# Products of odd chunks in the other half of the array, and key norms spread by a repeated stationary column

## The chip, the cores and the metric

The kernel runs on one core of a Trainium2 chip. The time is the device time of one launch in microseconds (us). Before the change three runs took 1141.73, 1145.06 and 1147.56 us; the median is 1145.06 us. A difference of about 0.5% (5.7 us) is what a measurement of this kernel can tell from no change.

Engines are named as the profile names them: PE is TensorE's matmul side and PEld its weight loads, DVE is VectorE, ACT is ScalarE, POOL is GpSimd, SP issues most of the DMAs. All of them work through their own instructions strictly in order.

## What is computed

The reference is a two-layer network on one sequence of 256 tokens of width 2048: an RWKV-7 layer, then an attention layer with compressed, selected and windowed keys. The change lies in the RWKV layer. Cut to what matters there:

```python
rkvz = jnp.einsum('nbtd,nde->nbte', mixed[:4], w_rkvz)
r, k, v, z = rkvz[0], rkvz[1], rkvz[2], rkvz[3]
kk = heads(k * k_k)
kk = kk / jnp.maximum(jnp.sqrt(jnp.sum(kk * kk, axis=-1, keepdims=True)), 1e-12)
k = k * (1.0 + (a - 1.0) * k_a)
o = wkv7_scan(rh, heads(decay), kh, vh, -kk, kk * ah)
```

`wkv7_scan` is a recurrence over the tokens with a 64 x 64 state for each of 32 heads. The kernel computes it in chunks of 64 tokens: four chunks (NCH = 4), and per head and chunk a 64 x 64 matrix of products between the normed, decayed keys and their scaled counterparts, of which a triangular inverse is needed.

## The kernel before

Weights come from HBM as fp32 pieces (`wraw`), and each is split into a high and a low part (`whi` by ACT at L211, `wlo` by DVE, some by POOL, at L190); three matmuls per weight block then give nearly fp32 products. PE is busy with these dense products almost throughout. A weight buffer has five places, so `whi` and `wlo` of a unit are made some four units ahead of the matmuls that read them, and not earlier than PE has let go of an old place.

The program runs in stages. First v, then one column block z0, then the sixteen key blocks k0 to k15 of 128 channels (two heads each), then z1 to z3, then the scan over the chunks together with the products for r. The change lies in the stage of the key blocks. Behind the dense products of key block j, a side chain `stage_k(j)` makes what the scan needs from it. In its order: two small matmuls for decay and gate (L689, L690); a copy and a square of the block (L695, L696) and the sums of the squares of the two heads by matmul into columns 256 to 259 of a PSUM bank `rn` (L699); `sst`, the floor of the sums, on DVE (L707); `rnt`, the power -1/2, on POOL (L708); then the norms have to be spread from one column per head over 64 partitions: ACT writes each norm 64 times side by side (`rnx`, L714, 128 x 256) and PE transposes that in two 128 x 128 blocks into `rn` (L717). DVE reads `rn` for `nk` (L729), then makes `at` (L730, a part of the tile `sp`) and `an` (L731). POOL makes the four parts of BK in `sp` (L736, L737). `sp` goes to HBM (`spd`, L739), PE makes eight 64 x 64 products, one per chunk and head (L744), ACT evicts them (`abs`, L746) and one DMA on SP writes them to HBM (`abd`, L747).

In the products, head 0 lies in partitions 0 to 63 and head 1 in 64 to 127, for the operands and for the output. So one product works in the upper left quarter of the array and the next in the lower right one.

When block 7 has been written, a side program `stage_t(0)` starts (`inverse_ops`): it loads eight blocks of products from `abd` (tile `invA`, two DMAs at L780) and computes triangular inverses with many small DVE operations, all of line L774 (tiles `invT`, `invM`, `invX`). The second half of the blocks follows in the scan. Another side program mixes the inputs for r (`mtmp` at L433, the two parts of `mx` at L426 and L427), also on DVE and ACT. z1 is closed by a tanh on ACT and a product on DVE (`zth`, L647), which frees a PSUM bank that z2 needs: z2 takes the two banks 2 and 0, and bank 0 is one of z1's.

Up to the scan the instructions are put in order by a scheduler that simulates the engines when the program is built: side chains are woven into the dense stream where it expects their inputs to be there. From the scan on, a planner written in the kernel sets the order.

Of the kernel before, what the change touches and what calls it, by code (L numbers as in the profile page):

```python
# [12 lines left out]
AF = mybir.ActivationFunctionType  # L13
# [211 lines left out]
def hybrid_kernel(ctx: ExitStack, tc: tile.TileContext, a: dict, out: bass.AP):  # L225
    nc = tc.nc
    V, S, G, PE = nc.vector, nc.scalar, nc.gpsimd, nc.tensor
# [147 lines left out]
    ident = C("ident")  # L375
# [286 lines left out]
    abd = dram.tile([16, NCH, 2, 128, 32], F32, name="abd")  # L662
# [11 lines left out]
    c3 = lambda x: x.rearrange("p (c t) -> p c t", c=NCH)  # L674

    def stage_k(j):
        PE, V, S, G = Ranked(nc.tensor, "skPE"), Ranked(nc.vector, "skE"), Ranked(nc.scalar, "skE"), Ranked(nc.gpsimd, "skE")
        yield lambda: j in kdone and (j < KLAG or (j - KLAG) in a1done)
        tmp = lambda name, bufs=2: kph.tile([128, T], F32, name=name, bufs=bufs)
        abs_ = tmp("abs")  # L680
# [17 lines left out]
        for tt in range(2):  # L698
# [11 lines left out]
        cum = tmp("cum")  # L710
        V.tensor_tensor_scan(cum, C("rst"), thw, 0.0, op0=OP.mult, op1=OP.add)
        yield 1000.0
        rnx = tmp("rnx")
        S.activation(rnx.rearrange("p (a b n) -> p a b n", a=2, b=2),  # L714
                     rnt[:, :, :, None].to_broadcast([128, 2, 2, 64]), AF.Copy)
        for tt in range(2):
            PE.transpose(rn[:, tt * 128:(tt + 1) * 128], rnx[:, tt * 128:(tt + 1) * 128], ident)  # L717
        sch.t += 215
        G.memset(pp[:, :, 0:1], 1.0)
        S.activation(pp[:, :, 1:], c3(cum), AF.Exp, scale=-DECAY)  # L720
# [19 lines left out]
        ab = accp("ab")  # L740
        for c in range(NCH):
            for h in range(2):
                r = slice(64 * h, 64 * h + 64)
                PE.matmul(ab[r, c * 64:c * 64 + 64], c3(at)[r, c, :], BK[r, c, h, :], start=True, stop=True)  # L744
        sch.t += 700
        S.activation(abs_, ab[:, :256], AF.Copy)  # L746
        nc.sync.dma_start(abd[j].rearrange("c k p s -> p (c k) s"), abs_.rearrange("p (n s) -> p n s", s=32))  # L747
        a1done.add(j)

    kacc = []  # L750
# [314 lines left out]
    def phase(U, c, p):  # L1065
# [5 lines left out]
        if p == 0:  # L1071
            if c == 0:
                removal(U, 0)
            else:
                for k, o in enumerate((px, O)):
                    for x, h in each:
                        PE.matmul(o[H(x, h), x], ARS[U % 2][x][R[h], k, c - 1, :], st[R[h], x, :], start=False, **mm)
        elif p == 1:
            for x, h in each:
                PE.matmul(pu[R[h], x], Yb[U % 2][H(x, h), x, c, :], XS[U][H(x, h), x, :], start=False, **mm)  # L1080
        elif p == 2:
            if c < NCH - 1:
                for x, h in each:
                    PE.matmul(pS[R[h], x], BKT[U % 2][x][:, c, h, :], uv[:, x, c, h, :], start=False, **mm)
            for x, h in each:
                PE.matmul(O[H(x, h), x], AMR[U % 2][:, h, x, c, :], uv[:, x, c, h, :], start=False, **mm)
            if c < NCH - 1:
                removal(U, c + 1)
        elif p == 3:
            XS[U] = scan.tile([128, 2, 64], F32, name="X", bufs=2)  # L1090
            S.activation(XS[U], px, AF.Copy)
        elif p == 4:
            for h in range(2):
                S.activation(uv[R[h], :, c, h, :], pu[R[h]], AF.Copy)
        elif p == 5:
            nxt = scan.tile([128, 2, 64], F32, name="S", bufs=3)
            if c == 0:
                V.tensor_copy(nxt, pS)
            else:
                V.tensor_tensor(nxt, SST[U][1], pS, op=OP.add)  # L1100
            SST[U] = (nxt, None)
        else:
            nxt = SST[U][0]
            dec = scan.tile([128, 2, 64], F32, name="sP", bufs=2)
            for x in range(2):
                S.activation(dec[:, x], nxt[:, x], AF.Copy, scale=PCH[U][:, x, c:c + 1])
            SST[U] = (nxt, dec)
# [880 lines left out]
```

## Time and profile before

| | |
|---|---|
| median of three runs | 1145.06 us (1141.73 to 1147.56) |
| the profiled execution, its own time | 1145.28 us |
| its span, first to last instruction | 1143.5 us |
| mean granted TensorE clock | 0.992 |
| PE, PEld busy | 1113.6 us, 962.9 us |
| DVE, ACT, POOL busy | 864.4 us, 715.3 us, 346.9 us |
| time of the DMA packets of SP's queue | 65.0% of 16 engines' span |

In the profile every instruction has its source line. An fp32 matmul stands as two records, a transpose as one. Matmuls are pipelined: a record's duration is longer than the step from one record's start to the next, and that step is what a matmul costs in a dense stream. "Idle before" is the time in which the engine stood before the instruction, with what ended it.

### The profile page before, as it was taken

To read this page: it belongs to the slowest core of one execution; us is meant where nothing else is said; L and a number is where in the kernel's file an instruction comes from. 1 tells how busy PE (TensorE), PEld (TensorE's weight loads), DVE (VectorE), ACT (ScalarE), POOL (GpSimd) and SP (SyncE) were. 2 spreads that over 40 slices of the span, in tenths; PEclk is the share of its full clock that TensorE was granted. 3 is DMA by queue.
4 is the path that set the end of the run, shared out by engine and by line. 5 is a ranking of instruction groups with operands and counts; after the bars stand their busy time and mean duration, and the time that the engine had idled before them with its cause. 6 is when DMAs were issued, how large, how long until landed. Compare 5 with 4: busy or idle time off the path is not lost.

```text
span 1143.5 us, 24949 instructions
## 1 busy us (share of the span) xinstructions
PE 1113.6 (97%) x9136; PEld 962.9 (84%) x9136; DVE 864.4 (76%) x1807; ACT 715.3 (63%) x1680; POOL 346.9 (30%) x443
## 2 busy tenths in 40 slices
PE   8999999999999999999999999999999999999997
PEld 7788899988688988888778888787889988888787
DVE  7999976779978986556666877675576888988564
ACT  5667777767655465556556766664666666666553
POOL 1400045554434365444110010100334344452212
PEclk9999999999999999999999999999999999999999
DMA  6568978885899978665457758585756453748462
GB/s 227 169 189 233 250 205 245 227 219 173 265 282 276 240 196 236 170 172 137 139 183 224 234 166 284 164 291 167 187 152 162 117 149 105 198 108 283 166 194 102
DMA packets 238522, 225.37 MB, mean 197 GB/s; under 512 B 57541, under 2 KB 184821, under 8 KB 238400
## 3 DMA queue, kind: packets, MB, share of 16 engines
q1 hardware_dynamic: 233120, 217.17, 65.0%
q0 software_dynamic: 5280, 6.61, 2.1%
q8 instruction: 72, 1.18, 0.5%
q14 instruction: 50, 0.41, 0.1%
HBM read 200.48 MB, written 23.10 MB: 196 GB/s over the span
## 4 chain that ended last, share of the span: by engine, by line
PE 62%; DVE 5%; DMA 2%; issue 2%; ACT 1%; POOL 1%; POOLq 0%; ACTq 0%; DVEq 0%
PE bank L576 9%; PE bank L577 9%; PE bank L579 9%; PE bank L601 5%; PE bank L1285 3%; PE bank L602 3%; PE bank L241 2%; DMA Yb<-yvd 2%; PE bank L1286 2%; PE bank L1287 2%; DVE wlo L190 2%; PE pair L1304 2%; PE pair L1306 1%; PE pair L1305 1%; PE pair L241 1%
## 5 line engine op out<-in xcount | busy, mean ns | idle before, releaser
L190 DVE TENSOR_TENSOR wlo<-wraw,whi 128x512 fp32r<-128x512 f32 (+2 forms) x616 | 448.9, 744 | 150.4 <-ACT whi L211 147.8
L211 ACT ACTIVATE whi<-wraw 128x512 fp32r<-128x512 f32 (+2 forms) x664 | 402.7, 620 | 232.9 <-PE bank L579 91.7
L577 PE MATMUL bank<-wlo,mx 128*128 128x512 f32 (+3 forms) x576 | 217.8, 380 | 3.5 <-DVE wlo L190 2.6
L579 PE MATMUL bank<-whi,mx 128*128 128x512 f32 (+3 forms) x576 | 215.0, 376 | 0.0
L576 PE MATMUL bank<-whi,mx 128*128 128x512 f32 (+3 forms) x576 | 186.5, 377 | 1.3 <-ACT whi L211 0.5
L577 PEld LDWEIGHTS bank<-wlo,mx 128*128 128x128 f32 x576 | 108.7, 189 | 22.8 <-DVE wlo L190 5.4
L576 PEld LDWEIGHTS bank<-whi,mx 128*128 128x128 f32 x576 | 107.9, 189 | 19.1 <-ACT mx L1869 1.2
L579 PEld LDWEIGHTS bank<-whi,mx 128*128 128x128 f32 x576 | 108.7, 189 | 16.2 <-POOL mx L1870 0.4
L190 POOL TENSOR_TENSOR wlo<-wraw,whi 128x512 fp32r<-128x512 f32 (+2 forms) x48 | 63.1, 1316 | 110.6 <-ACT whi L211 88.7
L601 PE MATMUL bank<-mx,whi 128*128 128x512 f32 x240 | 86.8, 398 | 0.0
L595 PE MATMUL bank<-mx,whi 128*128 128x256 f32 (+1 forms) x288 | 85.0, 295 | 0.3 <-ACT mx L426 0.3
L596 PE MATMUL bank<-mx,whi 128*128 128x256 f32 (+1 forms) x288 | 82.3, 286 | 0.0
L597 PE MATMUL bank<-mx,wlo 128*128 128x256 f32 (+1 forms) x288 | 81.7, 286 | 0.0
L1285 PE MATMUL bank<-mx,whi 128*128 128x256 f32 x256 | 81.6, 319 | 0.0
L577 PE MATMUL bank<-wlo,kvh 128*128 128x512 f32 x192 | 76.9, 401 | 0.0
L579 PE MATMUL bank<-whi,kvl 128*128 128x512 f32 x192 | 76.1, 396 | 0.0
L1286 PE MATMUL bank<-mx,whi 128*128 128x256 f32 x256 | 72.9, 285 | 0.0
L1287 PE MATMUL bank<-mx,wlo 128*128 128x256 f32 x256 | 72.8, 284 | 0.0
L602 PE MATMUL bank<-mx,wlo 128*128 128x256 f32 x256 | 70.6, 285 | 0.2 <-DVE wlo L190 0.2
L576 PE MATMUL bank<-whi,kvh 128*128 128x512 f32 x192 | 67.4, 396 | 0.0
L426 ACT ACTIVATE mx<-mtmp 128x256 fp32r<-128x256 f32 x96 | 38.7, 413 | 31.1 <-DVE mtmp L433 30.8
L595 PEld LDWEIGHTS bank<-mx,whi 128*128 128x128 f32 (+1 forms) x288 | 54.0, 187 | 2.2 <-ACT mx L426 0.7
(344 smaller groups left out, 2393.8 us busy)
## 6 DMA issues: line engine op xcount, KB each, us to landing
wraw<-in_a_w_rkvz_dram SPq DMA_DIRECT2D x128, 512.0 KB, 5.4
wraw<-in_kv_w_dram SPq DMA_DIRECT2D x48, 512.0 KB, 4.4
wraw<-in_b_w_in_dram SPq DMA_DIRECT2D x40, 512.0 KB, 4.2
wraw<-in_a_w_o_dram SPq DMA_DIRECT2D x32, 512.0 KB, 4.6
wraw<-in_b_w_o_dram SPq DMA_DIRECT2D x32, 512.0 KB, 3.9
spd<-sp SPq DMA_DIRECT2D x16, 642.0 KB, 5.1
wraw<-in_b_w_in_dram SPq DMA_DIRECT2D x24, 384.0 KB, 3.4
spl<-spd SPq DMA_DIRECT2D x14, 642.0 KB, 7.2
```

Of the source, the lines that this page charges most:

```text
L190: eng.tensor_tensor(lv, src, hv.bitcast(F32), op=OP.subtract)
L211: self.nc.scalar.activation(hv, src, AF.Copy)
L576: PE.matmul(o, mh[:, ts], wh[:, 0, :], start=k == ends[0], stop=False)
L577: PE.matmul(o, mh[:, ts], wl[:, 0, :], start=False, stop=False)
L579: PE.matmul(o, ml[:, ts], wh[:, 0, :], start=False, stop=k == ends[1])
L595: PE.matmul(o, wh[:, s, :], mh, start=k == 0 and first, stop=False, **kw)
L596: PE.matmul(o, wh[:, s, :], ml, start=False, stop=False, **kw)
L601: PE.matmul(o, wh[:, s, :], joint[nm, k], start=k == 0, stop=False, **kw)
L602: PE.matmul(o[:, :T], wl[:, s, :], mh, start=False, stop=False, **kw)
L1285: PE.matmul(o, wh[:, s, :], mh, start=k == 0, stop=False)
L1286: PE.matmul(o, wh[:, s, :], ml, start=False, stop=False)
L1287: PE.matmul(o, wl[:, s, :], mh, start=False, stop=k == NK - 1)
```

## The change

The norms are spread without a copy: PE takes a norm column of `rnt`, repeated 64 times by a zero step, as the stationary operand and the identity as the moving one. Four plain fp32 matmuls (two token halves, two heads), each to 64 partitions of `rn`, stand in place of one ACT operation and two transposes. The line numbers of the changed kernel are smaller by one from here to the products, and larger by four behind them.

The products of the odd chunks 1 and 3 are written to the other half of the partitions and to columns 384 to 511 of the bank `rn` instead of `ab`. The four quarters of the array are thus used in turn. The eviction becomes two ACT operations of 128 x 128, one per bank, and the write to HBM three DMAs, because the odd chunks' heads are swapped between partition halves. In HBM the chunks now stand in the order 0, 2, 1, 3; the loads that follow keep that order, and the one place in the scan that picks a chunk's inverse is given the matching index.

```diff
         yield 1000.0
-        rnx = tmp("rnx")
-        S.activation(rnx.rearrange("p (a b n) -> p a b n", a=2, b=2),
-                     rnt[:, :, :, None].to_broadcast([128, 2, 2, 64]), AF.Copy)
         for tt in range(2):
-            PE.transpose(rn[:, tt * 128:(tt + 1) * 128], rnx[:, tt * 128:(tt + 1) * 128], ident)
+            for h in range(2):
+                PE.matmul(rn[64 * h:64 * h + 64, tt * 128:(tt + 1) * 128], rnt[:, tt, h:h + 1].to_broadcast([128, 64]), ident,
+                          start=True, stop=True)
...
         for c in range(NCH):
             for h in range(2):
-                r = slice(64 * h, 64 * h + 64)
-                PE.matmul(ab[r, c * 64:c * 64 + 64], c3(at)[r, c, :], BK[r, c, h, :], start=True, stop=True)
+                r, o = [slice(64 * i, 64 * i + 64) for i in (h, h ^ (c % 2))]
+                pc = (ab, rn)[c % 2][o, (384 if c % 2 else 0) + c // 2 * 64:]
+                PE.matmul(pc[:, :64], c3(at)[r, c, :], BK[r, c, h, :], start=True, stop=True)
         sch.t += 700
-        S.activation(abs_, ab[:, :256], AF.Copy)
-        nc.sync.dma_start(abd[j].rearrange("c k p s -> p (c k) s"), abs_.rearrange("p (n s) -> p n s", s=32))
+        S.activation(abs_[:, 0:128], ab[:, 0:128], AF.Copy)
+        S.activation(abs_[:, 128:256], rn[:, 384:512], AF.Copy)
+        for c, src, dst in ((0, 0, 0), (2, 0, 64), (2, 64, 0)):
+            n = 64 if c else 128
+            nc.sync.dma_start(abd[j, c:c + 2, :, dst:dst + n].rearrange("c k p s -> p (c k) s"),
+                              abs_[src:src + n, 64 * c:64 * c + 128].rearrange("p (n s) -> p n s", s=32))
...
-                PE.matmul(pu[R[h], x], Yb[U % 2][H(x, h), x, c, :], XS[U][H(x, h), x, :], start=False, **mm)
+                PE.matmul(pu[R[h], x], Yb[U % 2][H(x, h), x, 2 * (c % 2) + c // 2, :], XS[U][H(x, h), x, :], start=False, **mm)
```

Since the scheduler sets the order, the change also moves instructions that it does not touch. From z2's first matmul into bank 0 on, PE's order is the same in both kernels; before that it differs in where the side chains stand. Three places follow.

The first is PE in the dense products of key block 5, where the products of block 3 and the norms of block 4 are woven in (each row is one instruction or several alike; `bank` with a number is an allocation of a PSUM bank, L595 to L597 are the dense products). Before:

```order
L744 MATMUL bank_2365<-sp 64x64
L597 MATMUL bank_2216<-mx_1582,wlo 128x256
L595 MATMUL bank_2216<-mx_1601,whi 128x256
L596 MATMUL bank_2216<-mx_1601,whi 128x256
L597 MATMUL bank_2216<-mx_1601,wlo 128x256
L744 MATMUL bank_2365<-sp 64x64 x7
L595 MATMUL bank_2216<-mx_1617,whi 128x256
```

And now:

```order
L744 MATMUL bank_2374<-sp 64x64
L744 MATMUL bank_2239<-sp 64x64
L595 MATMUL bank_2222<-mx_1640,whi 128x256
L596 MATMUL bank_2222<-mx_1640,whi 128x256
L597 MATMUL bank_2222<-mx_1640,wlo 128x256
L595 MATMUL bank_2222<-mx_1658,whi 128x256
L744 MATMUL bank_2374<-sp 64x64
L744 MATMUL bank_2239<-sp 64x64
L744 MATMUL bank_2374<-sp 64x64 x2
L744 MATMUL bank_2239<-sp 64x64 x2
L715 MATMUL bank_2367<-cst,rnt 64x128 x4
```

The eight products are split one and seven before, two and six now, and the norms' matmuls (L715) follow directly on the second part. Over the sixteen blocks, the products stand in one piece three times before and six times now, and the norms directly behind products six times now.

The second place is DVE where the first inverse starts; `sst` here is that of key block 9. The row `COPY invT<-invA` is the first DVE operation that reads the loaded products. Before:

```order
L711 SCALAR_TENSOR_TENSOR cum<-cst,thw 128x256
L190 TENSOR_TENSOR wlo<-wraw,whi 128x512
L726 TENSOR_TENSOR f<-ksb,f 128x256
L707 TENSOR_SCALAR sst<-bank_3002 128x4
L190 TENSOR_TENSOR wlo<-wraw,whi 128x512 x2
L774 COPY invT<-invA 128x16
L774 TENSOR_TENSOR invM<-invA,invT 128x32
```

And now:

```order
L711 SCALAR_TENSOR_TENSOR cum<-cst,thw 128x256
L190 TENSOR_TENSOR wlo<-wraw,whi 128x512
L725 TENSOR_TENSOR f<-ksb,f 128x256
L707 TENSOR_SCALAR sst<-bank_3026 128x4
L778 COPY invT<-invA 128x16
L778 TENSOR_TENSOR invM<-invA,invT 128x32
L778 TENSOR_TENSOR invX<-invA,invT 128x32
```

Two weight splits that stood ahead of the copy now stand behind it. On SP, the two loads of `invA` stood behind the write of the products, two small weight loads and the write of `spd`; now they stand behind the three writes and one load of `wraw`, and the write of `spd` behind them.

The third place is DVE where z1 is closed (`zth`, from z1's two banks). Before:

```order
L774 TENSOR_REDUCE invT<-invX 128x8x8
L190 TENSOR_TENSOR wlo<-wraw,whi 128x512
L433 SCALAR_TENSOR_TENSOR mtmp<-xx,prm,xn 128x256
L427 TENSOR_TENSOR mx_4287<-mtmp,mx_4287 128x256
L433 SCALAR_TENSOR_TENSOR mtmp<-xx,prm,xn 128x256
L190 TENSOR_TENSOR wlo<-wraw,whi 128x512
L774 TENSOR_TENSOR invX<-invT,invM 128x512
L190 TENSOR_TENSOR wlo<-wraw,whi 128x512
L433 SCALAR_TENSOR_TENSOR mtmp<-xx,prm,xn 128x256
L647 TENSOR_TENSOR zth<-bank_3811,zth 128x512
L647 TENSOR_TENSOR zth<-bank_3812,zth 128x512
```

And now:

```order
L433 SCALAR_TENSOR_TENSOR mtmp<-xx,prm,xn 128x256
L427 TENSOR_TENSOR mx_4335<-mtmp,mx_4335 128x256
L190 TENSOR_TENSOR wlo<-wraw,whi 128x512
L778 TENSOR_TENSOR invX<-invT,invM 128x1024
L190 TENSOR_TENSOR wlo<-wraw,whi 128x512 x2
L427 TENSOR_TENSOR mx_4371<-mtmp,mx_4371 128x256
L433 SCALAR_TENSOR_TENSOR mtmp<-xx,prm,xn 128x256
L190 TENSOR_TENSOR wlo<-wraw,whi 128x512
L427 TENSOR_TENSOR mx_4410<-mtmp,mx_4410 128x256
L647 TENSOR_TENSOR zth<-bank_3853,zth 128x512
L778 TENSOR_REDUCE invT<-invX 128x8x8
L647 TENSOR_TENSOR zth<-bank_3854,zth 128x512
```

The inverse has come further by the time z1 is closed. From the copy of the second place to the first `zth` of the third, DVE has 168 operations before and 176 now; the eight more are two splits `wlo`, two `mx`, two products of 128 x 1024 for the inverse and two of its reductions. PE's order at the start of z2 is alike in both: five weight blocks into bank 2 alone, then the same five into bank 0.

## The prediction

> **What bounds the kernel now.** I read the busy time by stretches first, then the chain of waits, then the timelines of the engines at the places that these name. Busy time by stretches, with the seams where DVE changes its state:
>
> ```profile
> 220.00:235.60 15.60, 15.60 (x138) 14.52 (x138) 8.33 (x14) 11.96 (x31) 7.74 (x10) 1.00 0.95 243
> 235.60:311.80 76.20, 70.29 (x502) 59.45 (x500) 75.47 (x170) 53.65 (x128) 35.74 (x43) 1.00 0.72 212
> 311.80:320.00 8.20, 8.14 (x29) 6.56 (x30) 8.15 (x14) 3.89 (x7) 5.15 (x10) 0.79 1.08 303
> 320.00:364.00 44.00, 44.00 (x236) 38.19 (x235) 34.71 (x82) 25.91 (x45) 12.48 (x20) 1.00 0.96 279
> ```
>
> The columns are the stretch, its length, then PE, PEld, DVE, ACT and POOL, the clock, and DMA. Up to 235.6 us PE is busy throughout and DVE about half. From 235.6 to 311.8 it is the other way round: DVE is busy 75.47 of 76.20 us, PE has 5.91 us without work. From 320 to 364, where the scan starts, PE is full again. So the change, which lies between 147 and 312 us, falls into two regimes. The chain of waits says the same of the seam at 311.8 (start, length, what):
>
> ```profile
> 296.31 0.60 DVE wlo L190
> 296.91 0.33 DVE mx L427
> ...
> 301.32 1.15 DVE wlo L190
> ...
> 306.68 0.60 DVE invT L774
> ...
> 311.20 0.61 DVE zth L647
> ...
> 311.86 0.63 PE bank L576
> ```
>
> The chain comes down DVE's queue, through splits, mixing and the inverse, to `zth`, which closes z1, and there passes to PE, whose first matmul of z2 into bank 0 waits for it. It then stays with PE. Where that chain in DVE's queue begins is shown by DVE's timeline:
>
> ```profile
> 229.12 0.69 DVE L190 TENSOR_TENSOR wlo<-wraw,whi 128x512 fp32r<-128x512 f32 x1 [0.26 <-ACT whi L211]
> 231.62 0.69 DVE L190 TENSOR_TENSOR wlo<-wraw,whi 128x512 fp32r<-128x512 f32 x1 [1.80 <-ACT whi L211]
> 235.64 0.19 DVE L774 COPY invT<-invA 128x16 f32<-128x16 f32 x1 [3.33 <-DMA invA<-abd]
> ```
>
> DVE stands for 3.33 us until the products of the first eight blocks have come back from HBM. From then on it never stands. Thus the time at which z2 can go on is the landing of `invA` plus all the work that the order puts on DVE between the copy and `zth`. That sum, not PE's, is what the change must be measured by.
>
> **The change, part by part.** First PE's small groups. What a group costs the dense stream is the step from the last dense matmul before it to the second one behind it, less two dense steps of 0.12 us:
>
> ```profile
> 170.79 0.28 PE L596 MATMUL bank<-mx,whi 128*128 128x256 f32 x1
> 171.00 0.33 PE L744 MATMUL bank<-sp 64*64 64x64 f32 x2
> ...
> 171.47 0.28 PE L595 MATMUL bank<-mx,whi 128*128 128x256 f32 x1
> ...
> 171.71 0.29 PE L597 MATMUL bank<-mx,wlo 128*128 128x256 f32 x1
> 171.93 0.68 PE L744 MATMUL bank<-sp 64*64 64x64 f32 x14
> ...
> 172.76 0.28 PE L596 MATMUL bank<-mx,whi 128*128 128x256 f32 x1
> ...
> 173.46 0.28 PE L596 MATMUL bank<-mx,whi 128*128 128x256 f32 x1
> 173.58 0.38 PE L717 MATMUL bank<-cst,rnx 128*128 128x128 f32 x2
> ...
> 173.92 0.28 PE L595 MATMUL bank<-mx,whi 128*128 128x256 f32 x1
> ```
>
> Products: 0.44 us for two records, 0.81 for fourteen, so 0.38 for going into the small shape and back and 0.031 a record. The two transposes cost 0.22 us. The scan has groups in the new shapes (L1077: 64 x 64 pieces in all four quarters; L1086: 128 partitions onto 64, 64 moving columns):
>
> ```profile
> 439.86 0.28 PE L1287 MATMUL bank<-mx,wlo 128*128 128x256 f32 x1
> 440.07 0.46 PE L1077 MATMUL pair<-S,ars 64*64 64x64 f32 x16
> ...
> 440.68 0.28 PE L1286 MATMUL bank<-mx,whi 128*128 128x256 f32 x1
> ...
> 450.14 0.28 PE L1287 MATMUL bank<-mx,wlo 128*128 128x256 f32 x1
> 450.35 0.45 PE L1086 MATMUL pair<-uv,amr 128*64 128x64 f32 x8
> ...
> 450.95 0.28 PE L1286 MATMUL bank<-mx,whi 128*128 128x256 f32 x1
> ```
>
> Sixteen records over four quarters cost 0.58 us, or 0.0125 a record beyond the 0.38. By the order, the sixteen blocks' products cost before 13 x 1.25 + 3 x 0.88 = 18.9 us (split in two, or whole), and now 10 x (2 x 0.38 + 16 x 0.0125) + 6 x 0.58 = 13.1 us: 5.8 us saved. The norms are eight records of the L1086 kind with 128 moving columns. L1086 costs 0.57, or 0.024 a record at 64 columns; I double it: 0.38 + 8 x 0.048 = 0.76 us. If a record is no dearer than at 64 columns it is 0.57; if halves don't overlap and each record takes a transpose's 0.11, it is 1.26. I take 0.76, the row of its own shape scaled by the columns. Six of the sixteen groups share one way of the switch with products, 6 x 0.19 = 1.1 us. So the norms go from 16 x 0.22 = 3.5 us to 16 x 0.76 - 1.1 = 11.1. On PE the change therefore costs 7.6 - 5.8 = 1.8 us, between -1.3 and +9.8.
>
> From 235.6 to 311.8 this is covered by PE's 5.91 us without work, and it would cost its full price if that cover were gone. Up to block 7, whose write the inverse waits for, it counts: about 7/16 of it, 0.8 us.
>
> ACT loses sixteen `rnx` and gains sixteen evictions; it is busy 53.65 of 76.20 us and sets nothing here.
>
> Second, the landing of `invA`. The eviction of block 7's products on ACT, then SP's own queue:
>
> ```profile
> 222.99 0.39 ACT L746 ACTIVATE abs<-bank 128x256 f32<-128x256 f32 x1 [0.90 <-PE bank L744]
> ...
> 223.90 0.54 SPq L747 DMA_DIRECT2D abd<-abs  x1
> ...
> 227.94 0.35 SPq L739 DMA_DIRECT2D spd<-sp  x1
> 229.05 1.21 SPq L780 DMA_DIRECT2D invA<-abd  x2
> DMA to landing us min/median/max: 3.3/5.3/8.4
> ```
>
> The last line is the view of `abd`'s writes. The load is issued 5.15 us after the write, as it must wait for the landing; then 6.59 us pass until the copy. Now: PE reaches the products of block 7 0.8 us later by the above and 0.5 us earlier by the order, where I count four dense matmuls fewer ahead of them; two evictions in place of one add about 0.2 us, an estimate: half of the 0.39 us; the last of three writes is issued two issues later, +1.1 us; it carries a quarter of the bytes and may land nearer the 3.3 us of the fastest write, for which I take half the distance, -0.9. Sum +0.7 us. The bounds are -1.8 (the write lands at once and the load, no longer behind the write of `spd`, gains as much again as the extra issues cost) and +2.5 (no gain anywhere, and SP held up by the load of `wraw` that now stands ahead). Behind the waiting load on SP stand that write of `spd` and the next weights; POOL waits for `spd` before it reuses `sp`, but has time, 35.74 us busy of 76.20.
>
> Third, and largest, DVE between the copy and `zth`. Eight operations more stand there now than before, and DVE has no free time to take them. Two of them are the splits that DVE did at 229.12 and 231.62, in time that it has free ahead of the copy; now they are behind it. Their prices:
>
> ```profile
> 280.59 1.21 DVE L774 TENSOR_REDUCE invM<-invX 128x64 f32<-128x1024 f32 x1
> 281.72 0.68 DVE L190 TENSOR_TENSOR wlo<-wraw,whi 128x512 fp32r<-128x512 f32 x1
> 314.65 1.22 DVE L774 TENSOR_TENSOR invX<-invT,invM 128x1024 f32<-128x1024 f32 x1
> 315.79 2.07 DVE L190 TENSOR_TENSOR wlo<-wraw,whi 128x512 fp32r<-128x512 f32 x3
> ```
>
> By steps: two splits at 0.60, two `mx` at 0.33 (both in the chain above), two products of 1024 at 1.14 (314.65 to 315.79), one reduction of 1024 at 1.13 and one of 512 at 0.60 (306.68). Together 1.20 + 0.66 + 2.28 + 1.73 = 5.9 us. The lower bound is 4.7, if the two splits still find a hole in DVE's queue; the upper is 6.9, with the slower steps that DVE shows beside POOL's work (1.15 for a split in places of the chain, 0.5 more for each of two).
>
> The sum: `zth`, and with it z2 in bank 0, moves by 5.9 + 0.7 = 6.6 us. PE by itself, 1.8 us later by its groups and with 5.91 us to spare, would be at that seam 4.1 us before its present time, so it doesn't decide. Behind the seam PE is full up to the scan and the chain stays with it, so nothing gives the time back; what the inverse has done early, DVE would have done in z2 in free time, 34.71 busy of 44.00 us. That gives 1145.28 + 6.6 = **1151.9 us** for the execution profiled, 0.2 us above the median of 1145.06, so about +0.6%.
>
> One rule of the Trainium skill speaks against the products: "TensorEngine Tiling (Array Packing)", Gotcha 1: PSUM Pressure, says that different row tiles cannot access the same PSUM bank simultaneously. Here both heads' rows still share a bank. L1077 writes the two halves of a bank from two row halves in the same way, so by that row the rule does not bite; its time would be that of the third rival, which gets a small chance for it.
>
> **The rivals.** (1) *PE decides, and nothing else.* If DVE had more slack than its busy time shows, the cost would be PE's 1.8 us: 1147.1 us. For it, PE is full up to 235.6 us; against it, the chain and the 75.47 us. (2) *Faster, by the shorter chain of the norms.* If PE decides, then what it waits for on that chain decides too, and the chain loses an ACT step (total, times, longest):
>
> ```profile
> PE bank L744 <- POOL sp L736: 2.7, 2, 2.1
> PE bank L717 <- ACT rnx L714: 1.8, 2, 1.3
> ```
>
> With both waits gone, 4.5 us, and the norms at their lower bound, -1.3 on PE, it would be 1145.28 - 5.8 = 1139.5 us. It is faster from the point where the waits that vanish outweigh PE's own +1.8. It needs DVE not to be the bound, and the profile says that it is. (3) *The quarters don't overlap.* If row halves that share a bank take turns, a record keeps its 0.031 us: 256 x 0.0185 = 4.7 us more on PE, 6.5 in all, still inside the cover. PE overtakes DVE only from 6.6 + 5.9 = 12.5 us on. With the norms at their upper bound as well it comes to 9.8 + 4.7 = 14.5; less the cover of 5.9 that is 8.6 at the seam, and 1153.9 us.
>
> **How the numbers follow.** DVE decides: 0.68, with 1148.5 to 1155 as its own range: 6.6 us, down to 2.9 by its lower bounds (4.7 - 1.8) and up to 9.4 by its upper ones. PE alone: 0.17. Faster: 0.08. Third rival: 0.07. The stretch at 311.8 with a clock of 0.79 follows DVE's starving of PE, and may come again or not: 8.2 x 0.21 = 1.7 us either way. For eight in ten I take 1144.5 to 1156. About 0.5%, 5.7 us, is what a measurement of this kernel can tell from no change, so slower begins at 1150.8: two thirds of the first case and most of the third, 0.50. Within 0.5%: 0.43. Faster: 0.07.
>
> **What would show it.** In the changed profile: the copy `invT<-invA` at 236 to 237 us, with more than 3.33 us of idle time before it; DVE without idle time from there to the first `zth` of z1 (now L651), and that near 318 us; PE's idle time before it over 5.91 us, by DVE's splits; products at about 0.0125 us a record and norms at 0.76 us a group. I am wrong if the first `zth` comes before 314 us, if DVE stands between the copy and it, or if PE rather than DVE is on the chain at that seam. If the span up to the scan is unchanged, the DVE count was the wrong measure; if it grows and the norms take over 1 us each, PE was.

## The result and the profile after

The changed kernel takes 1159.48 us in the median of 5 runs (1153.07 to 1160.03), the kernel before 1145.06 (1141.73 to 1147.56): the ratio is 1.0118, with a 95% interval of 1.0093 to 1.0143. It is slower by about 14 us, where 6.6 were forecast. The execution profiled took 1159.89 us, one of the longest of the five; its span is 1158.0.

Busy time by stretches, cut at the same events as before (columns as in the prediction): the copy `invT<-invA`, z1's close, and the start of z3.

```profile
220.00:234.50 14.50, 14.50 (x139) 13.52 (x138) 7.18 (x14) 10.28 (x28) 8.49 (x11) 1.00 0.76 212
234.50:316.20 81.70, 75.98 (x566) 63.99 (x564) 80.92 (x178) 56.20 (x137) 35.82 (x37) 0.98 0.68 197
316.20:325.00 8.80, 8.74 (x38) 7.24 (x39) 6.90 (x13) 5.32 (x9) 4.25 (x8) 1.00 1.01 281
325.00:341.50 16.50, 13.21 (x56) 10.05 (x54) 6.58 (x16) 6.21 (x11) 7.97 (x18) 1.00 1.02 277
341.50:345.40 3.90, 3.84 (x10) 3.04 (x11) 3.36 (x11) 1.89 (x3) 2.79 (x4) 0.56 0.73 205
```

From the copy to z1's close it is as before: DVE without idle time (80.92 of 81.70 us), PE 5.72 us without work. New is the fourth row: at the end of z2 PE stands for 3.3 of 16.5 us, and the fifth, where it then runs at a clock of 0.56. DVE's timeline of the changed kernel at the two places:

```profile
234.50 0.18 DVE L778 COPY invT<-invA 128x16 f32<-128x16 f32 x1 [3.42 <-DMA invA<-abd]
...
315.53 0.68 DVE L647 TENSOR_TENSOR zth<-bank,zth 128x512 f32<-128x512 f32 x1
316.13 1.21 DVE L778 TENSOR_REDUCE invT<-invX 128x64 f32<-128x1024 f32 x1
317.25 0.68 DVE L647 TENSOR_TENSOR zth<-bank,zth 128x512 f32<-128x512 f32 x1
...
339.94 0.18 DVE L778 COPY invT<-invA 128x16 f32<-128x16 f32 x1 [2.17 <-DMA invA<-abd]
...
340.81 0.68 DVE L647 TENSOR_TENSOR vt<-bank,vt 128x512 f32<-128x512 f32 x1
```

And the same of the kernel before, at the close of z2:

```profile
334.17 0.68 DVE L647 TENSOR_TENSOR vt<-bank,vt 128x512 f32<-128x512 f32 x1
...
340.23 0.18 DVE L774 COPY invT<-invA 128x16 f32<-128x16 f32 x1
```

Before, `vt`, which closes z2, stands ahead of the copy that starts the second inverse; now it stands behind it, and the copy waits for its load. The chain of waits of the changed kernel shows what hangs on it (start, length, what):

```profile
327.76 12.15 DMA invA<-abd
...
339.94 0.18 DVE invT L778
...
340.90 0.61 DVE vt L647
...
341.56 0.50 PE bank L576
```

PE's row there is:

```profile
341.56 0.50 PE L576 MATMUL bank<-whi,mx 128*128 128x512 f32 x1 [2.90 <-DVE vt L647]
```

So the time goes in four steps. In the middle of z2 the changed kernel is 2.8 us late. Of these, 1.1 were there already at its first matmul of L595, in code that the change does not touch (the same kernel profiled again, e8 below, began that 0.1 us early). `zth` was 4.4 and 5.5 late, but the half clock stretch behind that seam, 1.7 us, did not come. From there to z3 it loses 5.8 more: 0.9 with two short stands for splits, 3.2 at `vt` and 1.7 by the half clock. From the first G of the scan (G is the scan's first set of matmuls, L998, now L1002) to the first matmul of o, the layer's output product, it takes 182.2 us in place of 177.3, 4.9 more; and 1.0 more in all that follows.

### The profile page after: what moved, and what is told of

It reads as the page before. It is cut to its first block, busy times and chain, and to the rows that moved or that the text cites. A ratio compares the mean times of both kernels' runs of the same rounds, so it can differ in the third digit from the quotient of the medians.

```text
span 1158.0 us, 25213 instructions
## 1 busy us (share of the span) xinstructions
PE 1120.7 (97%) x9232; PEld 965.6 (83%) x9232; DVE 859.8 (74%) x1807; ACT 710.3 (61%) x1680; POOL 349.0 (30%) x443
## 4 chain that ended last, share of the span: by engine, by line
PE 72%; DVE 11%; DMA 6%; issue 4%; POOL 3%; ACT 3%; SPq 1%; ACTq 0%; POOLq 0%; DVEq 0%
PE bank L577 10%; PE bank L579 10%; PE bank L576 10%; PE bank L601 5%; DVE wlo L190 4%; PE bank L1289 3%; PE bank L602 2%; DMA Yb<-yvd 2%; PE bank L241 2%; PE bank L595 2%; PE bank L596 2%; PE bank L1290 2%; PE bank L1291 2%; PE bank L597 2%; DMA invA<-abd 2%
## 5 line engine op out<-in xcount | busy, mean ns | idle before, releaser
L595 PE MATMUL bank<-mx,whi 128*128 128x256 f32 (+1 forms) x288 | 85.7, 298 | 0.3 <-ACT mx L426 0.3
L597 PE MATMUL bank<-mx,wlo 128*128 128x256 f32 (+1 forms) x288 | 81.2, 286 | 0.0
L579 PE MATMUL bank<-whi,kvl 128*128 128x512 f32 x192 | 76.1, 396 | 0.0
L595 PEld LDWEIGHTS bank<-mx,whi 128*128 128x128 f32 (+1 forms) x288 | 54.6, 190 | 2.7 <-ACT mx L426 0.7
L596 PEld LDWEIGHTS bank<-mx,whi 128*128 128x128 f32 (+1 forms) x288 | 54.8, 190 | 1.7 <-issue 0.7
```

Of the source, the lines that this page charges most:

```text
L579: PE.matmul(o, ml[:, ts], wh[:, 0, :], start=False, stop=k == ends[1])
L595: PE.matmul(o, wh[:, s, :], mh, start=k == 0 and first, stop=False, **kw)
L596: PE.matmul(o, wh[:, s, :], ml, start=False, stop=False, **kw)
L597: PE.matmul(o, wl[:, s, :], mh, start=False, stop=k == NK - 1, **kw)
```

## The experiments

**Measures.** For each profile: the operations that the order puts on DVE from the copy to the first `zth` of z1, and the time between these two; *to G*, from the first matmul of L595 (32.86 us before) to the scan's first G; *scan*, from there to the first matmul of o; *rest*, from there to the start of the last matmul. Ratios are to the kernel before, run beside it, with 95% intervals.

| kernel | median us | ratio | operations, us to `zth` | to G | scan | rest |
|---|---|---|---|---|---|---|
| before | 1145.1 | 1 | 168, 75.5 | 332.5 | 177.3 | 592.6 |
| changed | 1159.5 | 1.0118 (1.0093 to 1.0143) | 176, 81.0 | 340.0 | 182.2 | 593.7 |
| changed again (e8) | 1157.1 | 1.0121 (1.0090 to 1.0153) | 176, 80.8 | 339.7 | 182.2 | 593.7 |
| norms alone (e1) | 1155.2 | 1.0110 (1.0069 to 1.0151) | 178, 82.7 | 341.4 | 177.2 | 593.6 |
| products alone (e2) | 1155.7 | 1.0111 (1.0067 to 1.0154) | 160, 69.8 | 338.3 | 182.3 | 592.9 |
| before, hold 16 (e3) | 1150.9 | 1.0061 (1.0035 to 1.0087) | 159, 70.8 | 337.1 | 177.9 | 592.7 |
| changed, hold 16 (e4) | 1153.2 | 1.0092 (1.0058 to 1.0125) | 161, 74.7 | 333.1 | 181.7 | 593.4 |
| before, hold 8 (e6) | 1142.8 | 1.0004 (0.9987 to 1.0021) | 165, 73.5 | 330.6 | 176.0 | 592.6 |
| changed, hold 8 (e5) | 1149.8 | 1.0057 (1.0031 to 1.0083) | 170, 76.1 | 334.2 | 180.7 | 593.8 |
| the same again (e16) | 1150.2 | 1.0059 (1.0035 to 1.0083) | 170, 77.5 | 331.9 | 180.3 | 594.0 |
| norms alone, hold 8 (e7) | 1151.4 | 1.0078 (1.0050 to 1.0106) | 171, 79.4 | 335.4 | 177.5 | 592.7 |
| e5 with one norm (e15) | 1152.3 | 1.0088 (1.0063 to 1.0113) | 171, 78.9 | 337.6 | 176.2 | 592.6 |
| e6 with three writes (e13) | 1142.7 | 1.0000 (0.9975 to 1.0025) | 165, 73.5 | 331.7 | 179.7 | 592.8 |
| e5, writes by ACT (e14) | 1150.6 | 1.0068 (1.0041 to 1.0094) | 169, 77.6 | 332.8 | 176.0 | 593.9 |
| e6, chunks' place (e9) | 1142.1 | 0.9992 (0.9973 to 1.0011) | 165, 73.4 | 330.0 | 175.1 | 592.8 |
| before, three Yb (e10) | 1144.2 | 1.0020 (1.0000 to 1.0040) | 168, 75.5 | 335.0 | 177.5 | 593.1 |
| e5, three Yb (e11) | 1149.0 | 1.0068 (1.0044 to 1.0092) | 170, 76.1 | 333.1 | 176.0 | 593.9 |
| second behind z2 (e12) | 1159.9 | 1.0143 (1.0116 to 1.0170) | 176, 81.0 | 337.2 | 180.4 | 592.9 |
| the same again (e18) | 1154.7 | 1.0109 (1.0093 to 1.0126) | 176, 80.8 | 337.5 | 181.1 | 592.7 |
| panels late (e17) | 1158.6 | 1.0132 (1.0111 to 1.0154) | 176, 80.8 | 342.9 | 184.6 | 593.8 |

A profile is one execution, and executions of one kernel differ: the kernel before ran from 1137.7 to 1147.7 us beside these runs. Differences of 2 us between single profiles are therefore not read as more than that, unless several agree.

### Each half alone

e1 is the kernel before with only the new norms:

```diff
-        rnx = tmp("rnx")
-        S.activation(rnx.rearrange(...), rnt[...].to_broadcast([128, 2, 2, 64]), AF.Copy)
         for tt in range(2):
-            PE.transpose(rn[:, tt * 128:(tt + 1) * 128], rnx[:, tt * 128:(tt + 1) * 128], ident)
+            for h in range(2):
+                PE.matmul(rn[64 * h:64 * h + 64, ...], rnt[:, tt, h:h + 1].to_broadcast([128, 64]), ident, ...)
```

> Only the norms by the repeated stationary column; products and their write as before. Theory O (the loss is the order in which DVE gets the inverse's pieces: 8 more of them ahead of z1's close, and the second inverse's copy ahead of z2's close): here 10 more operations stand between the first copy and z1's close, and the second copy stands 30 operations ahead of z2's close, so PE should stand there 3 us or more as in the changed kernel, z1's close 5 to 7 us late; 1157 to 1165 us. Theory P (the loss is PE's own dearer groups): norms cost +7.6 on PE and nothing is saved on products, part of it covered: 1147 to 1153 us. Theory S (part of the loss, 4.9 us between the start of r and its end, comes with the rearranged products in HBM): r takes as long as before, within 1 us.

e2 is the changed kernel with these lines back as before.

> Only the products in four quarters and two banks, with the three writes; norms by the copy and the transposes as before. Its order puts 160 operations between the first copy and z1's close (168 before, 176 in the whole change) and the second copy behind z2's close. O: z1's close comes 3 to 6 us earlier than before and nothing is lost at z2: 1138 to 1143 us. P: PE saves 5.8 us, 1139 to 1145. S: r takes about 4.9 us longer than before even here, as the products in HBM are rearranged, which gives 1143 to 1148; without S r is as long as before within 1 us.

Each half alone costs nearly as much as both (1.1%). That doesn't fit prices that add, one a saving: it points to the order, which each edit shifts. e1 came close to what O expected: z1's close is 5.7 us late, its second copy stands far ahead of z2's close, and it is 1.1% slower; but PE stands 2.5 us there where O had 3 or more, for splits behind the copy and not for `vt`, and 1155.2 us lie below O's range and above P's. e2 missed the time of all three expectations (only its scan, 182.3 us, is as long as S said). Its order at the closes was good, but its products stood in PE's queue where POOL was not ready. The waits of PE in e2 from 140 to 316 us, and SP's queue there:

```profile
PE bank L745 <- POOL sp L736: 7.3, 8, 2.1
...
PE bank L717 <- ACT rnx L714: 0.8, 1, 0.8
```

```profile
234.45 3.13 SPq L751 DMA_DIRECT2D abd<-abs  x3
238.22 0.35 SPq L739 DMA_DIRECT2D spd<-sp  x1
240.88 1.19 SPq L785 DMA_DIRECT2D invA<-abd  x2
```

The load of `invA`, issued at 229.05 us before, is issued at 240.88: the copy comes 10.7 us later, and this, not the number of operations behind it, moves z1's close by 5.0.

### Holding the first inverse behind z1's close

To move DVE's order without touching the key blocks, a copy of one column of z1's closed tile into the inverse's scratch tile is put ahead of the inverse's last operations. They then stand behind z1's close:

```diff
+                    if b == 0 and lv == 16 and i0 == 0:
+                        ops.append(("V", 1, None, lambda: V.tensor_copy(X[:, 0:1], closed[1][1][:, 0:1])))
```

As shown it stands ahead of the last 8 operations; put ahead of that whole level it holds 16. First with 16, in the kernel before and in the changed one.

> The kernel before, with the last level of the first inverse (16 of its operations, about 14 us of DVE) held behind z1's close by one copy of a single column, so that 159 in place of 168 operations stand between the copy and z1's close and the second copy stands 21 behind z2's close. O: DVE no longer decides at z1, most of PE's 5.91 us without work and the half clock at 312 us go: 1137 to 1141 us. P: DVE's order does not matter: 1144 to 1147.

> The changed kernel with the same hold: 161 operations between the copy and z1's close, the second copy 21 behind z2's close. O: both losses of the order go, what is left against the kernel before with the same hold is PE's own +1 to +3 us: 1138 to 1145 us, no stall of PE at the start of z3. P: it stays 12 to 15 us above the kernel before with the same hold. S: r is 4.9 us longer than in the kernel before with the same hold; without S within 1 us.

z1's close did come 3.2 us earlier in both, and in e4 PE no longer stands for `vt`: it stands 1.2 us for a late split, and its z3 runs 1.9 us ahead of the kernel before. But 16 is too many. The first inverse ends later, so the second does too, and it now stands in DVE's queue when the scan begins, where PE waits (2.4 us for a split in e3): e3 is 0.6% slower than the kernel before, and both numbers for it were wrong, O's and P's, as was O's for e4. Against each other the two kernels differ by 2.3 us (1153.24 to 1150.92), where O had said +1 to +3 and P 12 to 15; the intervals of the two ratios overlap. Then with 8, by which DVE's and POOL's order is that of the kernel before at both closes:

> The changed kernel with only the last 8 operations of the first inverse held behind z1's close. By its order 170 operations stand between the copy and z1's close (168 before, 176 in the change), the second inverse's copy stands 8 behind z2's close as before (6 ahead of it in the change), and POOL stores the first inverse behind the loads of the scan's first panels, as before. Theory O (the direct price is PE's dearer groups, 2 to 3 us; all else is the order at the closes of z1, z2 and on POOL): the start of r comes 2 to 4 us after the one of the kernel before instead of 8.6, no stall of PE at the start of z3; with a scan that lasts as long as before 1145 to 1149 us. Theory P (the loss is in the new groups themselves or in the three writes): no gain, 1155 to 1160. Theory S (the scan lasts 4.9 us longer because of the rearranged products): 1150 to 1154, with 182 us from the first G to the first matmul of o, where O has 177 to 179.

> The kernel before with the same hold, as the control: 165 operations between the copy and z1's close, the second copy 9 behind z2's close, POOL's order as before. The hold itself should cost or gain less than 3 us: 1140 to 1147 us. By O the changed kernel with the hold is 2 to 4 us above this one, by P 10 us or more.

> Only the norms by the repeated stationary column, with the same hold: 171 operations between the copy and z1's close, the second copy 8 behind z2's close, POOL's order as before (without the hold this part alone took 1155.2 us, with the second copy 30 operations ahead of z2's close and a stall of 2.5 us there). O: norms cost +7.6 us on PE, of which DVE covers a part at z1, and the stall is gone: 1146 to 1152 us. P: as without the hold, 1154 to 1157.

> The changed kernel once more, for a second profile of it. If what the scan lost (4.9 us from the first G to the first matmul of o, by four to six short waits for Yb and by stretches at half clock) belongs to the program, it comes again at the same places, within 1 us. If it belongs to the one execution that was profiled, the waits and the half clock stretches stand elsewhere and the scan is shorter by 2 us or more. The stall at the start of z3 (2.9 us for vt) belongs to the order and should come again within 1 us.

> The changed kernel with the hold of 8 operations once more. If the scan's 180.7 us belong to the program, it is 180 to 182.5 us again; if they belong to the execution that was profiled, it may be anything from 175 to 182. The time should be 1149.8 us within 2 us.

The control e6 is the kernel before (1.0004). The changed kernel falls from 1.0118 and 1.0121 to 1.0057 and 1.0059: half of its loss, some 7 us, is the order of the inverse, its stores and its second start. That contradicts P. It also leaves more than O had said: 7 us between e5 and e6, where O had 2 to 4. With the norms alone and the hold (e7) it is 1.0078, inside O's range; that the products save time beside it (1.0057) these intervals can't tell. The hold moves z1's close, POOL's stores and the second start together, so the 7 us are not divided among them. e8 shows the unheld change losing at the same places again: 5.9 us at the start of z3, 4.9 in the scan.

### The second inverse and z2's close

e12 holds the second inverse alone behind z2's close, e18 repeats it:

```diff
-        yield lambda: (8 * b + 7) in a1done
+        yield lambda: (8 * b + 7) in a1done and (b == 0 or 2 in closed)
...
+        if b:
+            op("V", 1, V.tensor_copy, flat[:, 0:1], closed[2][1][:, 0:1])
```

> The changed kernel with the second inverse alone held behind z2's close (the first is as in the change, 176 operations ahead of z1's close). Theory O: the 2.9 us in which PE stands for vt at the start of z3 and the half clock stretch behind it go, so r starts 4 to 6 us earlier than in the change (8.6 after the kernel before), that is 3 to 5 us after it; z1's close stays 4 to 6 us late. If the scan is as in the change, 1152 to 1156 us. If the stall is not from that copy, r starts as late as in the change, and 1157 to 1161 us.

> The changed kernel with the second inverse alone held behind z2's close, once more with more rounds. If its first profile (1153.7 us, r 3.7 us earlier than in the change) stands for the kernel, the median is 1153 to 1156 us; if its other times do, 1157 to 1161 us, and the hold of the second inverse gains nothing because it comes too late for the scan.

DVE in e12:

```profile
339.46 0.68 DVE L647 TENSOR_TENSOR vt<-bank,vt 128x512 f32<-128x512 f32 x1
...
340.77 0.15 DVE L781 COPY invT<-zt 128x1 f32<-128x1 f32 x1
...
346.06 0.14 DVE L781 COPY invT<-invA 128x16 f32<-128x16 f32 x1
```

The stall is gone, and both profiles reach G some 2.4 us sooner than the changed kernel (337.4 against 339.8 on average). Not 4 to 6: PE now waits for late splits at that place instead (1.0 and 0.8 us for `whi` in e12). The times are 1159.9 and 1154.7 us; they overlap with those of the change, so a gain in time by this hold alone is not shown. e17 leaves the copy where the change has it and takes away what loads beside it; the added lines stand behind z2's close:

```diff
-                for x in range(2):
-                    G.dma_start(SPL0[x][:, :SPW], spd[x])
...
+                V.tensor_copy(SPL0[x][:, 0:1], zt[:, 0, 0, 0:1])
+                nc.sync.dma_start(SPL0[x][:, :SPW], spd[x])
```

> The changed kernel, the order of the inverse as in the change (176 operations ahead of z1's close, the second copy ahead of z2's close), but the loads of the scan's first two panels stand behind z2's close (two copies of one column make them wait) and are issued on SP's queue. Theory L (the copy is late because its load shares the transfers with the panels): the load of invA lands in 5 to 8 us in place of 12.2, the copy is done before PE ends z2, and PE stands less than 1 us at the start of z3; r starts 4 to 6 us earlier than in the change, unless the panels are now late for the scan. Theory C (the copy's place in the queue alone): the stall of 2.9 us and its half clock stretch come again. In time, L gives 1152 to 1156 us, C 1157 to 1160.

L falls. With the panels away the load still lands 10.7 us after its issue, DVE stands at the copy for 6.28 us, and PE now starves for the splits queued behind it (a row of DVE, then of PE):

```profile
339.59 0.18 DVE L778 COPY invT<-invA 128x16 f32<-128x16 f32 x1 [6.28 <-DMA invA<-abd]
```

```profile
340.66 0.50 PE L577 MATMUL bank<-wlo,mx 128*128 128x512 f32 x1 [2.68 <-DVE wlo L190]
```

So it is not the panels but the place of the waiting copy in DVE's queue that costs, C; by e12 and e18 that place alone is worth some 2.4 us up to G. Why its load lands so late there (5.7 us before) stays open. In the six profiles that issue it between 323 and 331 us (changed, e1, e8, e12, e17, e18) it lands after 9.2 to 13.1 us, in those that issue it later after 3.8 to 8.8.

### The scan

Every profile so far with the products in quarters had a scan of 180.3 us or more, every one without had 178.0 or less. e9 puts the chunks' place in HBM alone into the kernel before with the hold, by its one eviction:

```diff
-        S.activation(abs_, ab[:, :256], AF.Copy)
+        S.activation(abs_.rearrange("p (o e n) -> p o e n", o=2, e=2),
+                     ab[:, :256].rearrange("p (e o n) -> p o e n", e=2, o=2), AF.Copy)
```

> The kernel before with the hold of 8 operations (whose scan took 176.0 us from the first G to the first matmul of o), and of the change only the place of the chunks in HBM: the eviction of the products swaps chunks 1 and 2, and the scan reads the odd chunks' slots accordingly. The order of every engine is that of the same kernel without it. Five profiles with the rearranged products had scans of 180.7 to 182.3 us, five without had 176.0 to 178.0. Theory S (the place of the chunks makes the scan longer): 180 to 183 us for the scan and 1145 to 1149 us in all. Theory W (the scan's length goes by how the 3.41 us stretches of the clock fall on its waits for Yb, and not by the place of the chunks): 175 to 178 us for the scan and 1140 to 1145 us, the same as without.

S falls: scan 175.1, ratio 0.9992. e10 and e11 give the scan a third Yb buffer (`Yb[U % 3]`, its load behind the phase of three pairs earlier), in the kernel before and in the changed one with the hold:

> The kernel before with three Yb buffers in the scan in place of two, so that the loads of Yb need not wait for the phase of two pairs earlier. PE stands 4.3 us in the scan for the landing of Yb and runs at half clock for two stretches of 3.41 us behind such waits (3.4 us lost). Theory W: waits and half clock go together, and 4 to 7 us are gained, 1136 to 1140 us, with a scan of 170 to 173 us. If instead another load is late next (A10 is loaded behind it on the same queue and has one buffer), the gain is under 2 us: 1140 to 1144.

> The changed kernel with the last 8 operations of the first inverse behind z1's close (1149.8 us so, scan 180.7 us) and three Yb buffers. Theory W: the scan loses its waits and half clock stretches and comes to within 1.5 us of the kernel before with three buffers, 170 to 174 us; the whole is then 2 to 5 us above that kernel: 1140 to 1144 us. Theory S: the scan stays 4 us longer than that of the kernel before with three buffers.

The waits for Yb went, and the time did not: 1.0020 and 1.0068, as without (1 and 1.0057). In both profiles PE stands once for 2.7 to 2.8 us for `X` of ACT instead. W's gain was wrong. e13 and e14 take the writes: three in place of one in e6, and those of e5 issued by ACT (`nc.scalar.dma_start`):

> The kernel before with the hold of 8 operations and, of the change, only the three writes of each block's products in place of one. DVE's and POOL's order are those of the same kernel with one write (1142.8 us, scan 176.0 us). Theory D (the 32 further transfers on SP's queue set the scan's transfers back and make it longer): scan 180 to 182.5 us, 1146 to 1150 in all. Theory N (the writes cost nothing, since SP and the transfers have time there): scan 175 to 178, 1140 to 1145.

> The changed kernel with the hold of 8 operations and its three writes issued on ACT's queue in place of SP's, so that SP's queue is shorter by 48 issues. Order at the closes as in the held kernel (169 operations before z1's close, second copy 8 behind z2's close). D: the scan returns to 175 to 178 us and the whole to 1143 to 1147 (1149.8 with the writes on SP). N: scan 180 to 182.5, 1148 to 1152.

By the times the three writes cost nothing (1.0000) and off SP's queue they gain nothing (1.0068), so D's forecast of the times falls. But the interval of e13 reaches 2.9 us to either side, and a smaller price would not be seen in it. The scans of the two profiles, 179.7 and 176.0 us, are close to what D said; but these are the longest of e13's ten executions (1147.14 us) and the shortest of e14's (1146.06).

What a scan is made of can be read. Take from each scan half of its time at half clock, as an estimate of what that cost. What is left is 175.3 to 177.8 us in the eleven profiles with three writes on SP's queue, e13 among them, and 173.4 to 174.5 in the seven with one write or with the writes on ACT (e14). With three Yb it is 172.4 and 172.6, whatever the writes. So some 2.5 us of the scan go with the three writes on SP's queue, and up to 6.8 with the stretches of 3.41 us at half clock, of which a scan has none to four. That rests on e13 and e14, one profile each, and how writes that end at 312 us reach into the scan is not shown; the cause stays open. Waits of PE in the changed kernel's scan

```profile
PE pair L1002 <- DMA Yb<-yvd: 5.6, 8, 1.3
PE pair L1012 <- issue: 0.8, 1, 0.8
```

against 4.3 us for Yb and no such "issue" before, and three stretches at half clock in place of two (four in e8).

### The price of the norms

e15 is e5 with half of the norms' matmuls; it leaves out the second head's norm:

```diff
-            for h in range(2):
-                PE.matmul(rn[64 * h:64 * h + 64, ...], rnt[:, tt, h:h + 1].to_broadcast([128, 64]), ident, ...)
+            PE.matmul(rn[:, tt * 128:(tt + 1) * 128], rnt[:, tt, 0:1].to_broadcast([128, 128]), ident, ...)
```

> The changed kernel with the hold of 8 operations, but with one stationary column of 128 copies for both heads in place of two of 64, so that each block has two matmuls of 128x128 for the norms instead of four of 128x64. It leaves out the second head's norm, which gets the first's. If the norms' matmuls are the direct price of the change (0.76 us a group against 0.22, 8.6 us over the sixteen, less what they share), PE's part up to z3 falls by 5 to 8 us and the whole comes to 1142 to 1146 us, no more than 0.3% over the kernel before. If the norms are hidden or their price is smaller, it stays at 1147 to 1151.

No gain: 1152.3 us, ratio 1.0088 against 1.0057 and 1.0059. At block 12 PE is 2.1 us ahead of e16, 1.1 of them since its first matmul of L595, and by the start of z1 it has lost the other 1.0 again. A half clock stretch at 249.5 us, which e16 does not have, cost it some 1.7 of that way; even without it the gain would have been under 2 us, where 5 to 8 were expected. The waits of PE from 140 to 312 us in e15:

```profile
PE bank L717 <- POOL rnt L711: 4.6, 2, 3.6
PE bank L745 <- POOL sp L736: 3.4, 4, 1.4
```

and in e16:

```profile
PE bank L718 <- POOL rnt L711: 2.9, 4, 1.5
PE bank L747 <- POOL sp L738: 1.4, 3, 0.8
```

8.0 against 4.3 us: what PE saves it stands for POOL's `rnt` and `sp`. A price on PE says little here where PE waits for POOL on either side of it. None of these kernels beats the kernel before.

## Why the prediction was right or wrong

**The bound at z1's close: right.** In the table the time from the copy to `zth` goes with the number of operations, from 70.8 us for 159 to 82.7 for 178: about 0.6 us an operation, whatever else was changed, since e15 with fewer matmuls on PE closes z1 within 0.5 us of e16. e4, at 74.7 for 161, is the farthest off.

**The term for DVE: right.** 8 operations more, +5.9 us forecast; 81.03 less 75.49 are 5.5, and 5.3 in both e8 and e18.

**The landing: wrong in sign, inside its bounds (-1.8 to +2.5) in the first profile.** +0.7 forecast, -1.1 measured (copy at 234.50), -2.5 in e8. SP's queue shows why:

```profile
224.76 1.70 SPq L750 DMA_DIRECT2D abd<-abs  x3
226.56 0.56 SPq L177 DMA_DIRECT2D wraw<-in_a_w_rkvz_dram  x1
227.92 1.19 SPq L784 DMA_DIRECT2D invA<-abd  x2
```

The load follows the issue of the first write by 3.2 us, where it was 5.15. Half the distance to the fastest landing was too little. Of the two signs given for the copy, one was wrong (234.50, not 236 to 237) and one right (3.42 us of idle time before it). Two more signs were wrong: `zth` came at 315.53, not near 318, and PE's idle time before it was 5.72 us, not over 5.91.

**The groups on PE: right.** The step over the norms alone and over twelve products:

```profile
157.95 0.28 PE L595 MATMUL bank<-mx,whi 128*128 128x256 f32 x1
158.16 0.66 PE L715 MATMUL bank<-cst,rnt 128*64 128x128 f32 x8
...
158.97 0.28 PE L597 MATMUL bank<-mx,wlo 128*128 128x256 f32 x1
...
164.07 0.28 PE L596 MATMUL bank<-mx,whi 128*128 128x256 f32 x1
164.28 0.45 PE L744 MATMUL bank<-sp 64*64 64x64 f32 x12
164.66 0.39 PE L597 MATMUL bank<-mx,wlo 128*128 128x256 f32 x1
164.88 0.28 PE L595 MATMUL bank<-mx,whi 128*128 128x256 f32 x1
```

Less 0.24 these are 0.78 (0.76 forecast) and 0.57 (0.53): the halves that share a bank, here in different partitions of it, do overlap, and the third rival falls. All groups from 140 to 340 us cost 50.6 us against 48.2, waits inside them included: +2.4, where 1.8 was forecast. With the order held, the four profiles of the changed kernel (e5, e16, e14, e11) reach G in 333.0 us on average, the three of the kernel before (e6, e13, e9) in 330.8: +2.2.

**The second rival, wrong and instructive.** The ACT step is gone, and PE waits as long as before, 3.0 for `rnt` and 1.6 for `sp`, 4.6 us where it was 4.5:

```profile
PE bank L715 <- POOL rnt L708: 3.0, 4, 1.6
PE bank L744 <- POOL sp L735: 1.6, 4, 0.8
```

The order moved the norms' matmuls forward by about what the chain had become shorter: in the first twelve blocks they stand 29 dense matmuls behind the sums of the squares on average, 33 before, which at 0.12 us is 0.5 us; an `rnx` took 0.41.

**The step that failed** is the one from the seam to the end: "nothing gives the time back; what the inverse has done early, DVE would have done in z2 in free time". Something was given back there (the half clock stretch), and much more was lost. What the inverse did early is part of what cost: as four more of its operations stand ahead of z1's close (70, 66 before), the order starts the second inverse ahead of z2's close, with a copy that waits for a load. That copy stands 6 operations ahead of `vt`, where it stood 8 behind. PE's order is the same there, DVE's is not; the row was not priced, since the prediction compared DVE's orders only up to z1. The missed terms are 5.8 us at the start of z3 (with the first inverse held, in e5 and e16, 0.8 to 1.5 from the middle of z2 to the same place), 4.9 in the scan and 1.0 behind it. With 2.8 up to the middle of z2 they make 14.5. That the order costs half of the loss is shown by the hold; of the scan's part its size and what it is made of are known, its cause is open, and so is that of the last 1.0.

## What to carry to other kernels

Where a scheduler sets the order, an edit is priced twice: by its own instructions, which rows of the trace give within a few tenths of a microsecond, and by what the new order puts ahead of every operation on which a full engine waits. Compare the orders at all such places down to the end of the kernel, and look above all for an instruction that waits for a load and has moved ahead of one that doesn't. To tell the two prices apart, hold the order alike in both kernels by a small true dependency, with a control; here that took back half of the loss at no cost.

## What the hardware showed that was not expected

PE's clock falls to half for single stretches of 3.41 us (some of 6.83), and each 3.41 at a clock of 0.50 costs 1.7 us of dense work. Between 20 us and PE's last matmul the 20 profiles have 56 such starts, and within a profile they lie whole multiples of 3.41 us apart. The stretch of 3.41 us ahead of it had PE busy for 2 to 79% of its time, in 54 of 56 cases for 70% or less; it need not be idle throughout. Two pairs in the kernel before, then two in the changed one (behind the five engines stand the clock, DMA's share and GB/s, so the clock is the third number from the end):

```profile
308.67:312.08 3.41, 2.14 (x7) 1.00 (x7) 3.41 (x7) 1.60 (x5) 0.77 (x2) 1.00 1.03 366
312.08:315.49 3.41, 3.41 (x9) 2.63 (x9) 3.37 (x7) 1.26 (x2) 3.31 (x7) 0.50 1.10 363
431.55:434.96 3.41, 2.12 (x45) 1.80 (x44) 0.20 (x1) 2.00 (x7) 1.07 (x4) 1.00 1.07 352
434.96:438.37 3.41, 3.41 (x34) 3.19 (x34) 0.00 (x0) 2.06 (x7) 0.00 (x0) 0.50 0.81 162
```

```profile
338.52:341.93 3.41, 0.51 (x3) 0.33 (x3) 1.92 (x10) 0.80 (x2) 0.13 (x1) 1.00 0.76 206
341.93:345.34 3.41, 3.41 (x10) 2.65 (x9) 2.87 (x9) 1.54 (x3) 2.66 (x4) 0.50 0.77 220
440.92:444.33 3.41, 2.33 (x56) 1.93 (x55) 0.28 (x1) 1.67 (x7) 0.79 (x4) 1.00 1.05 361
444.33:447.75 3.42, 3.42 (x23) 3.08 (x22) 0.00 (x0) 2.53 (x9) 0.36 (x1) 0.50 1.22 250
```

By these rows a wait of 1.1 us that falls whole into one stretch can cost 2.8, an estimate (1.1 and 1.7). The rule isn't sharp: in the same grid some 100 stretches with PE busy for less than 75% were followed by none. The Trainium skill, "TensorE: Matmul & The Clock Gate", section "What's actually happening", gives a free-running window of 3413 ns, which these distances bear out. Its section "Why this matters for your kernels" advises no gaps of PE over some 3 us; here half clock followed stretches with only 1.1 to 1.3 us without work, and the measurement decides.
